# Mixing a paged decode into a dense FFN: six steps per half cache, three score bursts, quarter and paired products

## The chip, the core and the metric

The kernel runs on one core of one Trainium2 chip. The time is the device time of one execution in microseconds. Three runs of the kernel before took 1327.28, 1329.06 and 1329.76 us; the median, 1329.06 us, is what a later time is compared with. The kernel is one launch that computes everything from inputs in HBM to outputs in HBM. Five engines work side by side, each on its own queue of instructions: TensorE (PE in the profile, with its weight loads as PEld), VectorE (DVE), ScalarE (ACT), GpSimd (POOL) and SyncE (SP), which issues most DMAs. A semaphore makes one engine wait for another.

## What is computed

One layer of a hybrid decoder for two groups of tokens with shared weights: a prompt of 512 tokens, and a sample group of 8 sequences with 4 new tokens each, which attends to 4096 cached positions in pages of 128. All values are float32.

```python
h = h + 0.5 * rmsnorm(swiglu(rmsnorm(h, g0), wg[0], wu[0], wd[0]), g1)     # first FFN, width 2816
z = rmsnorm(h, g2) @ w_in                # HGRN2 group (4 heads) and MLA group (4 heads)
o_h = gated linear recurrence over z;    o_m = latent softmax attention over z and the cache
h = h + rmsnorm(concat(o_h, o_m) @ w_out, g3)
h = h + 0.5 * rmsnorm(swiglu(rmsnorm(h, g4), wg[1], wu[1], wd[1]), g5)     # second FFN

swiglu(x, wg, wu, wd) = (silu(x @ wg) * (x @ wu)) @ wd
# the sample group's attention, per sequence and head, over cached and new keys
s = (q_lat @ c_kv.T + q_rope @ k_rope.T) * scale;   p = softmax(masked s);   o = p @ c_kv
```

A cached position has a latent row of 256 numbers (both key and value) and a rotary key of 64. The pages of one sequence lie scattered in a pool and are found through a page table. The eight caches together are 42 MB.

## The kernel before, in words

**Layout.** Activations are held transposed: 128 features on the partitions, tokens along the free axis. The 544 tokens (512 of the prompt, 32 of the sample group) are two parts, `x = 0` with 256 columns and `x = 1` with 288, the sample tokens at its end.

**Dense products.** Each float32 weight tile is split into a high and a low float32r part by `weight` (line 219): SyncE loads `wraw` (512 KB, three buffers), ACT casts the high part `wh` (L237), DVE subtracts for the low part `wl` (L238). From the start of the second FFN four `wh`/`wl` pairs are in rotation (`NW` and `WX`). A product of a 128 x 128 tile is then three matmuls, and `gemm` (line 249, its matmuls at L246) runs all k tiles of a weight into one PSUM bank named `acc`, of which there are four. `gemm_q` (line 256) does the same as a generator and stops after every second k tile.

**The FFN as a generator.** `ffn` (line 297) runs the width of 2816 (22 columns of 128) in chunks of 6, 6, 5 and 5 columns for the second FFN. For each column j it makes the gate product, the up product, the SwiGLU product on DVE and ACT (L318 to L321) and its split into `hh` and `hl` (L158, L159), and yields: 48 matmuls per step for one part. After a chunk's columns come eight down products, one per 128 rows of the output, each over the chunk's 6 or 5 k tiles (18 or 15 matmuls), and each yields. The last k tile of a down product is the column that the chunk made last. So part 0 of the second FFN (`gb`, line 1016) is 22 + 32 = 54 steps.

**The decode as a generator.** The caches are worked in 16 halves (`Half`, line 1072), two for each of the 8 sequences. For a half:

- `gather` (line 1078): four indirect DMAs on POOL's queue bring two groups of 128 x 8 latent rows (`craw`, 1 MB each, in six slots of old activations: ulb, uhb, ha, hb, mb, q0) and their rotary keys (`rraw`, four buffers).
- `turn` (line 1097): DVE turns the keys of both groups in 32 x 32 blocks into `kh` (L1102, L1103). `KHB = 2` buffers of 10 KB per partition: both hold one half.
- `score` (line 1106, matmuls at L1115): 80 small matmuls, ten j by eight, on quarters of the array (64 rows by 32 columns), each two in the trace; then the row maxima `mxd`, `mxh` on DVE.
- `peak` (line 1126, PE at L1128, then DVE), `weigh` (line 1135, the exponential on ACT at L1138), `place` (line 1140: the weights turned and copied into `pbuf`).
- `value` (line 1148, matmuls at L1154): 16 matmuls, two each in the trace, of the weights with the latent rows; and `gathered` (line 1160, L1165), every second half, to collect the result.

`decode` (line 1168) runs them as a pipeline over halves. In a round n it gathers half n, turns half n - 1, scores, peaks, weighs and places half n - 2, and makes the values of half n - 3, in four yields: the first five j of the scores; the last five j, the values and the gather; the peak and the whole turn; the weights.

**What sets the order.** Lines 1244 to 1256 mix the two generators: 43 steps of the FFN (`DRATE = 0.8` of 54) over 79 steps of the decode, in even proportion. That gives the order in which instructions are traced. A planner then puts each engine's queue in order: it goes by the traced order, and where an instruction would have to wait by its own estimate, it takes a later one that is ready. An engine then works off its queue strictly in that order. `decode_new` (line 1028), the attention to the new tokens themselves, is a third generator stepped along with the decode.

**Behind it.** The 11 FFN steps that are left (three columns and eight down products) fill gaps in the output projection of part 1: `FILL = (4, (7, 8, 9), (1, 2, 3, 4), 4)` gives 4 steps before it, one at each of three places in it, and 4 behind it (line 1355 on).

Of the kernel before, what the change touches and what calls it, by code (L numbers as in the profile page):

```python
# [8 lines left out]
F32 = mybir.dt.float32  # L9
# [8 lines left out]
P = 128  # L18
# [20 lines left out]
ROWS = 8  # L39
# [11 lines left out]
W0 = 0  # L51
JOBS = (0, 1, 2, 6, 7, 8, 3, 4, 5)
CQ, NST = (0, 0, 0, 3, 1), 3
FILL = (4, (7, 8, 9), (1, 2, 3, 4), 4)
PTB, PEB, QNB = 2, 3, 1
LEP, LXP, EB, XB = (), (), 2, 2
PAT = (2, 2, 2, 2, 2, 2, 2, 3, 4, 2, 2, 3, 2)
PATL = (2, 1, 2, 1, 2, 1, 2, 2, 3, 1, 1, 2, 1)
NW, WX = 2, 2
DRATE = 0.8  # L60
KHB = 2
LEVELS = (32, 16, 8, 4, 2, 1)
CH = 64

# [39 lines left out]
def hybrid_step_kernel(  # L104
# [148 lines left out]
        mm3(acc[:, :n], [((wh[:, k], wl[:, k]), (act_[0][:, k], act_[1][:, k])) for k in range(kt)])  # L253
        return acc[:, :n]

    def gemm_q(wt, act_):
        wh, wl, kt = wt
        acc = ps("acc", "acc")
        n = act_[0].shape[-1]
        for k in range(kt):  # L260
            if k and k % 2 == 0:
                yield
            for i, (a, b) in enumerate(((wh, act_[0]), (wh, act_[1]), (wl, act_[0]))):
                nc.tensor.matmul(acc[:, :n], a[:, k], b[:, k], start=k + i == 0, stop=k == kt - 1 and i == 2)  # L264
        return acc[:, :n]

    def wcols(w, k0, kt, c0, n=P):
        return w[k0 * P : (k0 + kt) * P, c0 : c0 + n].rearrange("(k p) f -> p k f", p=P)
# [28 lines left out]
    def ffn(i, n_post, xs, u, nxt=None, mid=None, late=None, fin=None, pre=()):  # L297
        pool = cur[-1]
        yield
        r2 = {x: u[x][2] for x in xs}  # L300
# [50 lines left out]
        if mid:  # L351
            mid()
        for p in ends:
# [659 lines left out]
    ffa = ExitStack()  # L1013
    wx.append(ffa.enter_context(scope("ffa")))
    seam = []
    gb = ffn(1, 5, (0,), u4, late=lambda: rstd_u(u4[0], 0), pre=seam)
    next(gb)

    with scope("dec"):
# [45 lines left out]
        pbuf = mk([P, 2, 2, ROWS, 32], F32, "pbuf")  # L1065
        nc.gpsimd.memset(pbuf, 0.0)
        NH2 = 2 * NB
        NS = 3 * NH2 + 11

        PTG = {"ulb": 0, "uhb": -1, "ha": -1, "hb": 1, "mb": 0, "q0": -1}  # L1070

        class Half:
# [21 lines left out]
                    self.craw.append(craw)  # L1094
                    self.rraw.append(rraw)

            def turn(self):
                self.kh = []
                for g in range(2):
                    kh = mk([P, ROWS, 10, 32], F32, "kh", KHB)  # L1100
                    for a in range(0, ROWS, 4):
                        nc.vector.transpose(kh[:, a : a + 4, :8].rearrange("p a j k -> p a (j k)"), self.craw[g][:, a : a + 4])  # L1102
                    nc.vector.transpose(kh[:, :, 8:].rearrange("p a j k -> p a (j k)"), self.rraw[g])  # L1103
                    self.kh.append(kh)

            def score(self, js):
                q = qbd[self.b % 2]
# [59 lines left out]

        def decode():
            H = {}
            for t in range(NS):  # L1170
                n, r = divmod(t, 3)

                def at(k):
                    return H.get(n - k)

                if n < NH2 and r == 0:
                    H[n] = Half(n)
                if r == 0:
# [5 lines left out]
                    if at(2):  # L1184
                        at(2).score(range(5, 10))
                    if at(3):
                        at(3).value(H.get(n - 4))
                    if n >= 3 and at(0):
                        at(0).gather()
                    yield  # L1190
                elif r == 1:
                    if at(2):
                        at(2).peak()
                    if at(1):
                        at(1).turn()
                    yield
                else:
                    if at(3):
                        at(3).gathered()
                    if at(2):  # L1200
                        at(2).weigh()
                    yield
                    if at(2):
                        at(2).place()
                H.pop(n - 5, None)

        def decode_end():
# [36 lines left out]
        next(ga)  # L1244
        na, nb = NS + (NS + 2) // 3, int((22 + 32) * DRATE)
        ia, ib = 1, 0
        while ia < na:
            if ia * nb <= ib * na:
                next(ga, None)
                next(gn, None)  # L1250
                ia += 1
            else:
                next(gb, None)
                ib += 1
        for _ in ga:
            pass
# [162 lines left out]
```

## Time and profile before

| what | value |
|---|---|
| median of three runs | 1329.06 us |
| the profiled execution's own time | 1329.72 us |
| its span, first to last instruction | 1327.9 us |
| granted TensorE clock, mean | 0.991 |
| decode and second FFN mixed | about 745 to 1019 us |
| first and last score matmul | 784.5 and 1007.5 us |
| instructions of scores, values | 2560, 512 matmuls |

How to read it: the page gives each engine's busy time and share of the span; busy tenths in 40 slices of 33 us; the chain of work that ended last; and the costliest groups of instructions. Rows of the views name line, engine, operation and tiles as `out<-in`. A matmul's duration is longer than its distance to the next, since matmuls overlap; what counts is the distance from start to start. "issue" is a wait for which the profile shows no semaphore. Span and profiled time differ by 1.8 us that lie outside the first and last instruction.

### The profile page before, as it was taken

Reading aid. Unit: us, or ns where it says so; the run is one execution under the profiler, and the core shown is the slowest. Engines: PE = TensorE matmul, PEld = TensorE weight load, DVE = VectorE, ACT = ScalarE, POOL = GpSimd, SP = SyncE. Lnnn points to the kernel's source line nnn. Section 1 sums busy time; section 2 is a strip of 40 time slices with the busy share of each in tenths; the row PEclk is TensorE's granted clock in tenths of the full one; section 3 lists DMA queues with packets and bytes.
Section 4 is the critical chain, followed back from the end, with each engine's and each line's share of the span. In section 5 each row is a group of like instructions: output and inputs, shape, how many; then the busy total and the mean of one; then the engine's idle time right before and its main releaser. Section 6 shows DMA issues by size and latency. Waiting matters only on the chain.

```text
span 1327.9 us, 30474 instructions
## 1 busy us (share of the span) xinstructions
PE 1285.0 (97%) x12696; PEld 1205.2 (91%) x12696; DVE 888.4 (67%) x1782; ACT 697.7 (53%) x1454; POOL 76.7 (6%) x79
## 2 busy tenths in 40 slices
PE   7999999999999999999999899999899999999997
PEld 7999999999999988888888787877788999999996
DVE  7553245434558887786766878989888768566664
ACT  6543244224456754445658654554445677554454
POOL 0000000000000000000000413323210000000000
PEclk9999999999999999999999999999899999999998
DMA  6223232233244313233232869968768545656452
GB/s 187 84 84 92 82 94 81 82 95 95 76 131 128 110 52 97 81 87 115 74 96 77 313 202 285 312 213 312 256 212 262 153 134 166 180 152 181 140 167 70
DMA packets 280552, 192.87 MB, mean 145 GB/s; under 512 B 12765, under 2 KB 271422, under 8 KB 275550
## 3 DMA queue, kind: packets, MB, share of 16 engines
q1 hardware_dynamic: 271968, 147.85, 38.3%
q0 software_dynamic: 7168, 41.95, 8.4%
q8 instruction: 100, 1.64, 0.5%
q10 hardware_dynamic: 1278, 1.12, 0.3%
q14 instruction: 38, 0.31, 0.1%
HBM read 181.22 MB, written 9.67 MB: 144 GB/s over the span
## 4 chain that ended last, share of the span: by engine, by line
PE 83%; DVE 8%; ACT 4%; issue 2%; DMA 2%; SPq 0%; DVEq 0%; ACTq 0%
PE acc L246 61%; PE acc L264 9%; PE s L1115 3%; PE o L1154 2%; DVE kh L1102 2%; PE s L919 1%; DVE wl L238 1%; ACT wh L237 1%; PE pa L658 1%; PE zx L551 1%; DMA wraw<-w_u 1%; PE pr L179 1%; DMA xt<-x_p 1%; DVE ssq L173 0%; DMA wraw<-w_o 0%
## 5 line engine op out<-in xcount | busy, mean ns | idle before, releaser
L237 ACT CAST wh<-wraw 128x1024 fp32r<-128x1024 f32 (+3 forms) x255 | 248.4, 976 | 330.7 <-PE acc L246 266.8
L238 DVE TENSOR_TENSOR wl<-wraw,wh 128x1024 fp32r<-128x1024 f32 (+3 forms) x255 | 288.6, 1133 | 147.5 <-ACT wh L237 146.8
L246 PE MATMUL acc<-uhb,wh 128*128 128x288 f32 x768 | 228.3, 297 | 0.8 <-ACT uhb L195 0.8
L246 PE MATMUL acc<-ulb,wh 128*128 128x288 f32 x768 | 227.8, 297 | 0.0
L246 PE MATMUL acc<-uhb,wl 128*128 128x288 f32 x768 | 226.3, 295 | 1.2 <-DVE wl L238 1.2
L246 PE MATMUL acc<-uha,wh 128*128 128x256 f32 x768 | 220.6, 288 | 4.0 <-ACT wh L237 2.5
L246 PE MATMUL acc<-uha,wl 128*128 128x256 f32 x768 | 217.3, 284 | 1.8 <-DVE wl L238 1.7
L246 PE MATMUL acc<-ula,wh 128*128 128x256 f32 x768 | 217.4, 284 | 0.6 <-DVE ula L196 0.6
L246 PEld LDWEIGHTS acc<-uha,wh 128*128 128x128 f32 x768 | 145.6, 190 | 9.1 <-ACT wh L237 3.3
L246 PEld LDWEIGHTS acc<-uha,wl 128*128 128x128 f32 x768 | 145.5, 190 | 3.0 <-DVE wl L238 3.0
L246 PEld LDWEIGHTS acc<-uhb,wl 128*128 128x128 f32 x768 | 145.0, 189 | 1.7 <-DVE wl L238 1.7
L246 PEld LDWEIGHTS acc<-ula,wh 128*128 128x128 f32 x768 | 145.5, 190 | 1.1 <-DVE ula L196 1.0
L246 PEld LDWEIGHTS acc<-uhb,wh 128*128 128x128 f32 x768 | 144.7, 188 | 1.6 <-ACT uhb L195 1.0
L246 PEld LDWEIGHTS acc<-ulb,wh 128*128 128x128 f32 x768 | 144.7, 188 | 0.1
L246 PE MATMUL acc<-hlb,wh 128*128 128x288 f32 x317 | 93.8, 297 | 0.0
L246 PE MATMUL acc<-hhb,wh 128*128 128x288 f32 x317 | 93.4, 297 | 0.0
L246 PE MATMUL acc<-hhb,wl 128*128 128x288 f32 x317 | 92.9, 294 | 0.0
L246 PE MATMUL acc<-hha,wh 128*128 128x256 f32 x297 | 87.0, 293 | 5.5 <-ACT hha L158 4.2
L246 PE MATMUL acc<-hla,wh 128*128 128x256 f32 x297 | 84.5, 285 | 1.1 <-DVE hla L159 1.1
L246 PE MATMUL acc<-hha,wl 128*128 128x256 f32 x297 | 84.5, 285 | 0.0
L321 DVE TENSOR_TENSOR sil<-sil,acc 128x256 f32<-128x256 f32 (+1 forms) x88 | 38.2, 436 | 49.5 <-PE acc L246 47.4
L320 DVE TENSOR_TENSOR sil<-sil,sit 128x256 f32<-128x256 f32 (+1 forms) x88 | 38.5, 440 | 43.0 <-ACT sit L295 42.7
(476 smaller groups left out, 2767.4 us busy)
## 6 DMA issues: line engine op xcount, KB each, us to landing
wraw<-w_g SPq DMA_DIRECT2D x66, 512.0 KB, 4.0
wraw<-w_u SPq DMA_DIRECT2D x66, 512.0 KB, 3.8
wraw<-w_in SPq DMA_DIRECT2D x24, 512.0 KB, 3.8
wraw<-w_d SPq DMA_DIRECT2D x32, 384.0 KB, 3.8
wraw<-w_d SPq DMA_DIRECT2D x32, 320.0 KB, 3.3
wraw<-w_o SPq DMA_DIRECT2D x16, 512.0 KB, 4.1
wraw<-w_d SPq DMA_DIRECT2D x16, 448.0 KB, 3.7
wraw<-w_d SPq DMA_DIRECT2D x8, 512.0 KB, 4.0
```

The lines of the kernel that those rows point to most:

```text
L179: nc.tensor.matmul(pr[:, :n], ones, acc, start=True, stop=True)
L237: nc.scalar.copy(wh[:, :kt], w[:, :kt])
L238: nc.vector.tensor_tensor(wl[:, :kt], w[:, :kt], f32(wh[:, :kt]), op=ALU.subtract)
L246: nc.tensor.matmul(out, a, b, start=n == 0, stop=n == last)
L264: nc.tensor.matmul(acc[:, :n], a[:, k], b[:, k], start=k + i == 0, stop=k == kt - 1 and i == 2)
L320: nc.vector.tensor_tensor(s, s, t, op=ALU.mult)
L321: nc.vector.tensor_tensor(s, s, up[x], op=ALU.mult)
L551: nc.tensor.matmul(z, w[a][:, k], U[1][b][:, k], start=k + n == 0, stop=k == KD - 1 and n == 2)
L658: nc.tensor.matmul(pa[es, c * 32 : (c + 1) * 32].rearrange("p (n m) -> p n m", m=m), kx[:, cs], up(qx[:, cs]), start=True, stop=True, skip ...
L1102: nc.vector.transpose(kh[:, a : a + 4, :8].rearrange("p a j k -> p a (j k)"), self.craw[g][:, a : a + 4])
L1115: nc.tensor.matmul(self.s[r][c * 32 : c * 32 + 32, :P], q[rs, j], kh, start=j == 0, stop=j == 9, skip_group_check=True)
L1154: nc.tensor.matmul(o[g : g + 32, :R], self.p[:, c, a], self.craw[c][:, a], start=i + c == 0 and a < 4, stop=i + c == 2 and a >= 4, skip_gr ...
```

## The change

The edits, as one change:

- `decode` has six yields in a round instead of four: scores of three, three and four j, each its own step; the values and the gather; the peak; the weights. `turn` takes a group: group 0 in the step of the second score burst, group 1 in the step of the peak. In the first three rounds the gather stands in the first step, as before.
- `KHB` goes from 2 to 3. The scratch that holds POOL's DMA descriptors is set to 4096 bytes per partition (16384 by default), so 12288 bytes of each partition are free for other tiles; a buffer of turned keys has 10240.
- `gemm_q` takes a step size, and `ffn` a mode `fine`, used for part 0 of the second FFN alone. In it the gate and the up product each yield in the middle (after 4 of 8 k tiles, 12 matmuls) and at their end: four yields per column.
- In `fine`, except in the last chunk, the first two down products are made side by side by the new `gemm_2`: all k tiles but the last of the first, then of the second, a yield, then the last k tile of each.
- The mixing loop runs 6 x 19 = 114 decode steps and `NDEC = 100` FFN steps of the 120 that there are now; `decode_new` steps with every second decode step. 20 FFN steps stay for later, which are the same three columns and eight down products as before: `FILL` begins with 13 instead of 4.

```diff
-FILL = (4, (7, 8, 9), (1, 2, 3, 4), 4)
+FILL = (13, (7, 8, 9), (1, 2, 3, 4), 4)
-DRATE = 0.8
-KHB = 2
+NDEC = 100
+KHB = 3
...
-    def gemm_q(wt, act_):
+    def gemm_q(wt, act_, step=2):
...
-            if k and k % 2 == 0:
+            if k and k % step == 0:
                 yield
...
+    def gemm_2(wts, act_):
+        kt = wts[0][2]
+        n = act_[0].shape[-1]
+        accs = [ps("acc", "acc")[:, :n] for _ in wts]
+        for ks in (range(kt - 1), (kt - 1,)):
+            for (wh, wl, _), acc in zip(wts, accs):
+                for k in ks:
+                    for i, (a, b) in enumerate(((wh, act_[0]), (wh, act_[1]), (wl, act_[0]))):
+                        nc.tensor.matmul(acc, a[:, k], b[:, k], start=k + i == 0, stop=k == kt - 1 and i == 2)
+            if len(ks) > 1:
+                yield
+        return accs
...
-                ga = {x: gemm(wg_, u[x]) for x in xs}
+                ga, up = {}, {}
+                for x in xs:
+                    ga[x] = (yield from gemm_q(wg_, u[x], 4)) if fine else gemm(wg_, u[x])
+                if fine:
+                    yield
...
-                up = {x: gemm(wu_, u[x]) for x in xs}
+                for x in xs:
+                    up[x] = (yield from gemm_q(wu_, u[x], 4)) if fine else gemm(wu_, u[x])
...
-                wts = {d: pre.pop(0) if pre else weight([wcols(w_d[i], f0, nf, d * P)], nf, len(grp) > 1) for d in grp}
+                if fine and not last and grp[0] == 0:
+                    accs = yield from gemm_2([weight([wcols(w_d[i], f0, nf, d * P)], nf) for d in (0, 1)], (hh[xs[0]], hl[xs[0]]))
+                elif fine and not last and grp[0] == 1:
+                    accs = accs[1:]
+                else:
+                    accs = None
+                wts = None if accs else {d: pre.pop(0) if pre else weight([wcols(w_d[i], f0, nf, d * P)], nf, len(grp) > 1) for d in grp}
...
-                        acc = gemm(wts[d], (hh[x], hl[x]))
+                        acc = accs[0] if accs else gemm(wts[d], (hh[x], hl[x]))
...
-                yield
+                if not accs or grp[0] == 0:
+                    yield
...
-    gb = ffn(1, 5, (0,), u4, late=lambda: rstd_u(u4[0], 0), pre=seam)
+    gb = ffn(1, 5, (0,), u4, late=lambda: rstd_u(u4[0], 0), pre=seam, fine=True)
...
-            def turn(self):
-                self.kh = []
-                for g in range(2):
-                    kh = mk([P, ROWS, 10, 32], F32, "kh", KHB)
...
+            def turn(self, g):
+                if g == 0:
+                    self.kh = []
+                kh = mk([P, ROWS, 10, 32], F32, "kh", KHB)
...
         def decode():
             H = {}
-            for t in range(NS):
-                n, r = divmod(t, 3)
+            for n in range(NH2 + 3):
...
+                for r, js in enumerate((range(3), range(3, 6), range(6, 10))):
                     if at(2):
-                        at(2).score(range(5))
-                    if n < 3 and at(0):
+                        at(2).score(js)
+                    if r == 0 and n < 3:
                         at(0).gather()
+                    if r == 1 and at(1):
+                        at(1).turn(0)
                     yield
...
+                if at(3):
+                    at(3).value(H.get(n - 4))
+                if n >= 3 and at(0):
+                    at(0).gather()
+                yield
+                if at(2):
+                    at(2).peak()
+                if at(1):
+                    at(1).turn(1)
+                yield
+                if at(3):
+                    at(3).gathered()
+                if at(2):
+                    at(2).weigh()
+                yield
+                if at(2):
+                    at(2).place()
...
-        na, nb = NS + (NS + 2) // 3, int((22 + 32) * DRATE)
...
+        na, ib = 6 * (NH2 + 3), 0
+        for ia in range(na):
+            next(ga)
+            if ia % 2:
                 next(gn, None)
-                ia += 1
-            else:
-                next(gb, None)
+            while ib * na < (ia + 1) * NDEC:
+                next(gb)
                 ib += 1
...
-    nc = _bacc.Bacc("TRN2", target_bir_lowering=False, num_devices=1)
+    nc = _bacc.Bacc("TRN2", target_bir_lowering=False, num_devices=1, dynamic_dma_scratch_size=4096)
```

More of the change, by code (lines that the diff above doesn't have):

```diff
@@ L295, in sigmoid, with ffn @@
         nc.scalar.activation(out, out, AF.Exp, scale=-1.0)
-    def ffn(i, n_post, xs, u, nxt=None, mid=None, late=None, fin=None, pre=()):
+    def ffn(i, n_post, xs, u, nxt=None, mid=None, late=None, fin=None, pre=(), fine=False):
         pool = cur[-1]
@@ L1067, in hybrid_step_kernel @@
         NH2 = 2 * NB
-        NS = 3 * NH2 + 11
         PTG = {"ulb": 0, "uhb": -1, "ha": -1, "hb": 1, "mb": 0, "q0": -1}
@@ L1095, in gather @@
                     self.rraw.append(rraw)
-            def turn(self):
-                self.kh = []
-                for g in range(2):
-                    kh = mk([P, ROWS, 10, 32], F32, "kh", KHB)
[L1101 to L1104, printed above, removed]
+            def turn(self, g):
+                if g == 0:
+                    self.kh = []
+                kh = mk([P, ROWS, 10, 32], F32, "kh", KHB)
+                for a in range(0, ROWS, 4):
+                    nc.vector.transpose(kh[:, a : a + 4, :8].rearrange("p a j k -> p a (j k)"), self.craw[g][:, a : a + 4])
+                nc.vector.transpose(kh[:, :, 8:].rearrange("p a j k -> p a (j k)"), self.rraw[g])
+                self.kh.append(kh)
             def score(self, js):
@@ L1169, in decode @@
             H = {}
-            for t in range(NS):
-                n, r = divmod(t, 3)
+            for n in range(NH2 + 3):
                 def at(k):
                     return H.get(n - k)
-                if n < NH2 and r == 0:
+                if n < NH2:
                     H[n] = Half(n)
-                if r == 0:
+                for r, js in enumerate((range(3), range(3, 6), range(6, 10))):
                     if at(2):
-                        at(2).score(range(5))
-                    if n < 3 and at(0):
+                        at(2).score(js)
+                    if r == 0 and n < 3:
                         at(0).gather()
+                    if r == 1 and at(1):
+                        at(1).turn(0)
                     yield
[L1184 to L1196, printed above, removed]
-                else:
[L1198 to L1204, printed above, removed]
+                if at(3):
[15 more added lines that the diff above has]
+                    at(2).place()
                 H.pop(n - 5, None)
@@ L1243, in hybrid_step_kernel @@
         ga, gn = decode(), decode_new()
-        next(ga)
-        na, nb = NS + (NS + 2) // 3, int((22 + 32) * DRATE)
[L1246 to L1249, printed above, removed]
+        na, ib = 6 * (NH2 + 3), 0
+        for ia in range(na):
+            next(ga)
+            if ia % 2:
                 next(gn, None)
-                ia += 1
-            else:
-                next(gb, None)
+            while ib * na < (ia + 1) * NDEC:
+                next(gb)
                 ib += 1
```

## The prediction

> **What bounds the kernel now.** First the page: its busy rows, slices and chain.
>
> ```profile
> span 1327.9 us, 30474 instructions
> PE 1285.0 (97%) x12696; PEld 1205.2 (91%) x12696; DVE 888.4 (67%) x1782; ACT 697.7 (53%) x1454; POOL 76.7 (6%) x79
> ...
> PE   7999999999999999999999899999899999999997
> ...
> PE 83%; DVE 8%; ACT 4%; issue 2%; DMA 2%; SPq 0%; DVEq 0%; ACTq 0%
> ```
>
> PE sets the end: 83% of the chain. PE's work is not reduced by this change (the same matmuls run), so the only things to win are its idle time, its lost clock and the cost of changing between kinds of work. POOL's gathers and the decode lie in slices 23 to 31, so next the table by stretches, with the whole stage in which decode and the second FFN are mixed (745 to 1019) and its two slowest-clocked pieces.
>
> ```profile
> 745.00:1019.00 274.00, 254.40 (x4394) 217.66 (x4392) 239.25 (x527) 139.91 (x364) 66.26 (x59) 0.98 0.80 264
> 880.00:900.00 20.00, 17.68 (x284) 14.63 (x282) 15.93 (x39) 10.92 (x30) 4.23 (x4) 0.91 0.64 201
> 940.00:960.00 20.00, 17.22 (x276) 14.22 (x275) 15.17 (x32) 8.91 (x23) 4.54 (x4) 0.83 0.79 262
> ```
>
> The columns are length, PE, PEld, DVE, ACT and POOL busy, clock, DMA share, GB/s. In 274 us PE is idle 274 - 254.4 = 19.6 us, and a clock of 0.98 costs another 5.5. This is all the stage holds for PE. DVE is busy 239.25 us, leaving 34.75 free: it stands close behind PE. DMA engines are busy 0.80 of the time. Then PE's waits there (740 to 1030):
>
> ```profile
> PE s L1115 <- issue: 8.4, 6, 2.8
> PE acc L246 <- ACT wh L237: 2.5, 3, 1.8
> PE acc L246 <- ACT hha L158: 2.3, 3, 1.7
> PE s L1128 <- DVE mxh L1124: 1.6, 4, 0.8
> PE acc L246 <- issue: 1.3, 1, 1.3
> PE acc L246 <- DVE hla L159: 1.1, 2, 0.6
> PE acc L246 <- DVE wl L238: 1.0, 2, 0.8
> ...
> PE o L1154 <- issue: 0.6, 1, 0.6
> ```
>
> Half of it, 8.4 + 1.3 + 0.6 = 10.3 us, is "issue": no semaphore explains it. The chain of waits shows where, and the DMA views what moves then (whole run; 745 to 784; 925 to 950):
>
> ```profile
> 836.52 1.86 PE o L1154 x32
> ...
> 850.64 2.40 PE s L1115 x160
> ...
> 925.26 2.38 PE s L1115 x111
> 927.64 2.48 issue
> 930.13 0.42 PE s L1115 x7
> ...
> 935.32 5.78 PE acc L246 x48
> 941.10 2.16 PE s L1115 x143
> 943.26 2.78 issue
> ```
>
> ```profile
> q8 instruction: 100, 1.64, 0.5%
> ```
>
> ```profile
> q8 instruction: 2, 0.03, 0.3%
> ```
>
> ```profile
> q8 instruction: 4, 0.07, 1.1%
> ```
>
> A score matmul takes 2.40/160 = 15 ns, a dense one 5.78/48 = 120 ns. PE's code comes as 100 packets of 16.4 KB for 2 x 12696 instructions: one block is 127 load and matmul pairs, 15 us of dense work but 1.9 us of scores. A half has 160 score matmuls and 32 value matmuls in one stretch, and the gap opens after 110 to 140 of them. I read "issue" as the wait for the next block, in a DMA system 80% busy.
>
> [...]
>
> **The change, part by part.** *Scores in three bursts (24, 24 and 32 matmuls, each two in the trace: 48, 48, 64) with a piece of dense work between, and dense products in halves of 12 matmuls.* Six steps per half, 19 halves, 114 steps for 100 pieces: 0.88 piece a step. From the first score to the end of the values PE now issues 160 + 32 + 4 x 0.88 x 12 = 234 pairs, in 160 x 0.015 + 1.9 (values, the row of 1.86) + 42 x 0.12 = 9.3 us, so a block lasts some 5 us instead of 1.9; the stalls show that a block needs at most about 1.9 + 2.8 = 4.7. The waits go away, and the clock lost after the longest of them: 20 x (1 - 0.83) = 3.4 us. Together 10.3 + 3.4 = 13.7; bounds 0 and 13.7. I take 80%, since a step without a piece (12%) joins two bursts: -11.0.
>
> [...]
>
> *First two down products side by side.* At each of the three seams inside the stage the first product stops at its last k, whose input is the newest SwiGLU column:
>
> ```profile
> 887.70 0.28 PE L246 MATMUL acc<-hha,wl 128*128 128x256 f32 x1
> 889.66 0.39 PE L246 MATMUL acc<-hha,wh 128*128 128x256 f32 x1 [1.68 <-ACT hha L158]
> 890.69 0.49 PE L246 MATMUL acc<-hla,wh 128*128 128x256 f32 x1 [0.64 <-DVE hla L159]
> ```
>
> Now 15 matmuls of the second product (12 in the last chunk) stand ahead of it, 15 x 0.12 = 1.8 us. The waits on hha and hla are 2.3 + 1.1 = 3.4 us, the clock after them 20 x (1 - 0.91) = 1.8. The longest (2.32) keeps 0.5; I take -2.9 and half the clock, -0.9: -3.8, bounds 0 and -5.2. Price: two weight pairs held instead of one, of four.
>
> *More turns between dense and decode work.* One such turn, a half whose keys come late:
>
> ```profile
> 898.10 0.28 PE L246 MATMUL acc<-hha,wl 128*128 128x256 f32 x1
> 898.31 0.41 PE L1115 MATMUL s<-kh,q 64*32 64x128 f32 x4
> 898.65 0.39 PE L246 MATMUL acc<-hha,wh 128*128 128x256 f32 x1
> ```
>
> From start to start 0.55, less one dense pitch 0.12, less four scores 0.06: 0.37 us; the clean x160 stretch pays it once, halves split by late keys five times. I count 4 x 0.88 = 3.5 turns a half after, about 2.7 before (between one and five, nearer one): 0.8 x 16 x 0.3 = +4; bounds 0 (splits vanish) and (3.5 - 1) x 16 x 0.37 = +15.
>
> *Third kh buffer, turn in two parts.* DVE's work, from its groups in 745 to 1018, and the gathers' landing after issue (740 to 1030):
>
> ```profile
> L1103 DVE STREAM_TRANSPOSE kh<-rraw 128x512 f32<-128x512 f32 x32 | 22.2, 693 | 0.0
> L1102 DVE STREAM_TRANSPOSE kh<-ulb 128x1024 f32<-128x1024 f32 x12 | 14.8, 1234 | 1.4 <-PE s L1115 1.4
> ```
>
> ```profile
> rraw<-pool_r,idx POOLq DMA_INDIRECT x32, 7.0
> ...
> ha<-pool_c,idx POOLq DMA_INDIRECT x5, 7.5
> ...
> uhb<-pool_c,idx POOLq DMA_INDIRECT x5, 8.9
> ```
>
> One turn of both groups is 4 x 1.23 + 2 x 0.69 = 6.3 us; in two parts, 3.2 each, other DVE work passes between. The first part no longer waits for the previous scores (the 1.4 above is such a wait). It covers PE's 1.6 on mxh at best. But the gather stands in step 4 and the first turn in step 2 of the next half, four steps of about 274/19/6 = 2.4 us = 9.6 us, against 7.5 to 8.9 us of landing: the slack is about 1 us. On DVE's queue weight lows, SwiGLU products and maxima stand behind a turn that waits, and PE stands behind those. I take 0; bounds -1.6 and +23 (a rival below).
>
> *Finer mix.* Before, 43 pieces go into 79 steps, 2.2 a half, of 48 x 0.12 = 5.8 or 18 x 0.12 = 2.2 us; now 5.3 a half, of 1.4 or 2.2. The first score stands behind 12 x 0.88 / 4 = 2.6 gate and up columns instead of 8 x 43/79 = 4.4, and the first weights meet the first gathers harder. PE's waits on wh and wl, 2.5 + 1.0 = 3.5, may go or double: 0, bounds -3.5 and +3.5. The pieces left after the stage hold the same matmuls (13 + 3 + 4 quarter or whole steps for 4 + 3 + 4): 0; cover is PE's own queue.
>
> *Smaller descriptor scratch.* POOL's issues:
>
> ```profile
> L1093 POOL DMA_INDIRECT rraw<-pool_r,idx x32 | 40.2, 1258 | 66.0 <-DVE kh L1103 57.9 <-DVE q L1166 3.4 <-issue 2.3
> ```
>
> POOL idles 66 us before these alone, so even a doubled issue (another 40 us) is covered: 0. Were the cover gone it would delay the landing, the same rival.
>
> **The sum.** -11.0 - 3.8 + 4 = -10.8. The profiled execution took 1329.72 (span 1327.9 and 1.8 around it), 0.66 over the median 1329.06; so 1318.9 for it and 1318.3 on the median. I say 1318, range of this case 1311 to 1325.
>
> **Rivals.** *All waits go* (0.14): issue, clock, seams, mxh and the start, 13.7 + 5.2 + 1.6 + 3.5 = 24.0 of the 25.1 that the stage holds, with +3 for turns: 1329 - 21 = 1308. For it: DVE's 34.75 us free. Against: DVE would have to be 239/253 = 95% busy without ever holding PE up.
>
> *The bursts change nothing* (0.14): the issue gaps are not code blocks, or the planner lets bursts run together as it does today with two half scores (x160 above). Then -3.8 + 4 = 0: 1329. [...] Against: gaps of the same place and size, always inside scores or values.
>
> *DVE waits for the gathers* (0.26): with a buffer free early, the planner puts the first turn behind the second turn of the half before (step 5) rather than at its own place. That is 2.4 + 3.2 = 5.6 us after the gather's issue, where the latents land after 7.5 to 8.9 and the key rows, issued one POOL instruction (1.26) later, after 1.3 + 7.0 = 8.3. With 8.6: 3 us of waiting at the head of DVE's queue. DVE has 34.75/19 = 1.8 us free a half, 1.25 in a stage 11 us shorter. In 10 of the 13 halves gathered inside the loop: 10 x (3 - 1.25) = +17.5, less 10.8: +7, 1336. It decides from a wait of about 2.3 us a half. For it: DVE's load. Against: none of DVE's waits in the stage before names a gather.
>
> **How the numbers follow.** The forecast has 0.46. Under 0.2% (2.7 us) a measurement of this kernel can't tell a change. Faster: 0.46 + 0.14 + 0.04 of the third case = 0.64; same: 0.10 of it; slower: 0.26. The range 1306 to 1338 takes in the forecast, most of the first and half of the last rival, about 0.82.
>
> **What would show it.** Right: issue waits before L1115 and L1154 under 3 us together, no 20 us stretch of the stage below 0.95, hha and hla waits under 1.5, score groups of 48 to 64 in PE's order, the stage 10 us shorter. Wrong: a DVE wait before kh on a gather, more than 64 turns, issue gaps that stay though the bursts are apart.

## The result, and the profile after

The changed kernel took 1336.09 us in the median (1332.37 to 1338.02), the kernel before 1329.06: a ratio of 1.0047 with a 95% interval of 1.0034 to 1.006. It is slower, by 6.2 us on that ratio; the forecast was 10.8 us faster. The execution that was profiled took 1332.37 us, the fastest of these runs, so its trace shows a smaller loss than the median.

The page after, first its span and engines, then the slices of PE and the chain of work that ended last:

```profile
span 1330.6 us, 30465 instructions
PE 1286.0 (97%) x12696; PEld 1204.8 (91%) x12696; DVE 888.4 (67%) x1782; ACT 698.3 (52%) x1454; POOL 77.0 (6%) x79
...
PE   7999999999999999999999888989999999999997
...
PE 77%; DVE 11%; DMA 6%; ACT 4%; issue 2%; SPq 0%; DVEq 0%; ACTq 0%; POOLq 0%
```

The same matmuls run, and DVE's and ACT's totals are the same within 0.6 us. What differs is the chain: PE had 83% of it and has 77; DVE went from 8 to 11 and DMA from 2 to 6. The end is now reached by way of transfers and DVE more often. The stage in which decode and the second FFN are mixed, and its two slowest-clocked slices (columns as in the prediction):

```profile
745.00:1019.00 274.00, 254.79 (x4361) 218.04 (x4361) 236.09 (x510) 138.45 (x353) 67.24 (x59) 0.98 0.79 260
800.00:820.00 20.00, 15.75 (x266) 13.43 (x267) 13.83 (x33) 8.38 (x24) 5.13 (x5) 0.91 0.68 225
820.00:840.00 20.00, 17.25 (x281) 15.11 (x280) 15.80 (x34) 9.65 (x28) 5.77 (x4) 0.91 0.90 303
```

PE's busy time in these 274 us was 254.40 and is 254.79, at the same clock: no idle time was won, and 33 fewer matmuls fit in (4361 for 4394). PE's waits in the stage (740 to 1045; total us, times, longest):

```profile
PE s L1152 <- DVE mxh L1148: 9.7, 5, 3.0
PE acc L264 <- DVE wl L238: 4.2, 4, 2.6
PE s L1139 <- issue: 2.7, 2, 2.5
PE s L1139 <- ACT q L1162: 1.8, 1, 1.8
...
PE o L1178 <- issue: 0.2, 1, 0.2
```

The row that the change aimed at did what was forecast: "issue" fell from 10.3 us to 2.7 + 0.2, and the waits on hha and hla (3.4) are gone from the list. In their place stands the wait for the row maxima (L1148, before L1124), 1.6 before and 9.7 now, and that for wl, 1.0 before and 4.2 now. Both are made by DVE, though DVE is less busy (236.09 for 239.25). So the next question is what DVE's queue waits for, and behind it ACT's. First ACT before, then ACT after, then DVE after:

```profile
ACT wh L237 <- DMA wraw<-w_u: 7.9, 2, 6.3
```

```profile
ACT wh L237 <- DMA wraw<-w_u: 17.8, 6, 4.3
...
ACT wh L237 <- DMA wraw<-w_d: 11.1, 8, 3.6
...
ACT wh L237 <- DMA wraw<-w_g: 4.8, 5, 1.3
```

```profile
DVE wl L238 <- ACT wh L237: 13.9, 12, 3.1
...
DVE kh L1126 <- DMA ha<-pool_c,idx: 2.3, 3, 1.3
DVE kh L1126 <- DMA ulb<-pool_c,idx: 2.2, 2, 1.1
DVE kh L1126 <- DMA mb<-pool_c,idx: 1.8, 2, 1.0
```

Two kinds of waiting on transfers stand behind this. ACT stands 33.7 us before casts whose raw weights have not landed; before, its waits that name a weight load were 7.9 + 2.3 + 0.7 = 10.9 us (w_u, w_d, w_g), so this kind is not new but three times as large. And DVE stands 6.3 us before turns whose latents have not landed, where no wait of DVE's named a gather before. The chain of waits shows how each reaches PE (start, length, what). First the gather of half 8:

```profile
877.99 7.80 DMA mb<-pool_c,idx
...
885.81 1.25 DVE kh L1126
...
894.23 1.24 DVE kh L1126
895.47 0.37 DVE mxd L1146 x2
895.84 1.15 DVE kh L1126
896.99 0.05 DVE mxh L1148
...
897.09 0.80 PE s L1152 x2
```

The transfer ends at 885.79 and the first turn starts 0.02 us later; the next turn, 894.23, is in DVE's queue ahead of the maxima and partly between their two steps, and PE's peak at 897.09 has waited for it. Then the end of the decode:

```profile
1011.39 6.78 DMA wraw<-w_u
...
1018.27 1.05 ACT wh L237
...
1019.34 1.23 DVE wl L238
1020.57 0.41 DVE mxd L1146 x2
...
1021.00 0.17 DVE mxh L1148
...
1021.22 0.49 PE s L1152 x2
```

Here a wait "for the maxima" is a weight that came late: its low part stands ahead of the maxima in DVE's queue, and DVE stood 3.08 us before it (1016.26 to 1019.34), though the scores that the maxima read had ended at 1015.44. One name in PE's list, two causes; the experiments separate them.

### The profile page after: what moved, and what is told of

Its sections match the earlier page's. It is cut to its first block, busy times and chain, and to the rows that moved or that the text cites. A ratio compares the mean times of both kernels' runs of the same rounds, so it can differ in the third digit from the quotient of the medians.

```text
span 1330.6 us, 30465 instructions
## 1 busy us (share of the span) xinstructions
PE 1286.0 (97%) x12696; PEld 1204.8 (91%) x12696; DVE 888.4 (67%) x1782; ACT 698.3 (52%) x1454; POOL 77.0 (6%) x79
## 4 chain that ended last, share of the span: by engine, by line
PE 77%; DVE 11%; DMA 6%; ACT 4%; issue 2%; SPq 0%; DVEq 0%; ACTq 0%; POOLq 0%
PE acc L246 52%; PE acc L264 13%; DVE wl L238 2%; DVE kh L1126 2%; DMA wraw<-w_u 2%; PE s L944 1%; ACT wh L237 1%; PE s L1139 1%; DMA mb<-pool_c,idx 1%; PE pa L683 1%; PE o L1178 1%; DMA wraw<-w_g 1%; PE zx L576 1%; DVE pbuf L1170 1%; PE pr L179 1%
## 5 line engine op out<-in xcount | busy, mean ns | idle before, releaser
L264 PE MATMUL acc<-uha,wh 128*128 128x256 f32 x528 | 159.4, 302 | 1.4 <-ACT wh L237 0.9
L264 PE MATMUL acc<-uha,wl 128*128 128x256 f32 x528 | 150.2, 285 | 4.2 <-DVE wl L238 4.2
L264 PE MATMUL acc<-ula,wh 128*128 128x256 f32 x528 | 150.5, 286 | 0.6 <-DVE ula L196 0.6
L246 PE MATMUL acc<-uha,wh 128*128 128x256 f32 x416 | 118.2, 284 | 1.0 <-DVE sil L336 1.0
L246 PE MATMUL acc<-uha,wl 128*128 128x256 f32 x416 | 117.6, 283 | 0.8 <-DVE wl L238 0.8
L246 PE MATMUL acc<-ula,wh 128*128 128x256 f32 x416 | 117.5, 282 | 0.0
L264 PEld LDWEIGHTS acc<-uha,wh 128*128 128x128 f32 x528 | 101.0, 191 | 14.8 <-issue 11.3
L264 PEld LDWEIGHTS acc<-uha,wl 128*128 128x128 f32 x528 | 100.7, 191 | 5.4 <-DVE wl L238 5.2
L264 PEld LDWEIGHTS acc<-ula,wh 128*128 128x128 f32 x528 | 101.1, 192 | 2.0 <-DVE ula L196 1.0
L246 PEld LDWEIGHTS acc<-uha,wh 128*128 128x128 f32 x416 | 78.5, 189 | 1.4 <-DVE sil L336 1.2
L246 PEld LDWEIGHTS acc<-uha,wl 128*128 128x128 f32 x416 | 78.4, 188 | 1.4 <-DVE wl L238 1.4
```

What stands on the lines that cost most here:

```text
L246: nc.tensor.matmul(out, a, b, start=n == 0, stop=n == last)
```

## Experiments

The theory after this reading: (1) with an even mix, three raw weight buffers (`wraw`) let the dense loads arrive late among the gathers; (2) the third buffer of turned keys lets the planner put the first turn where the gather has barely landed. Rivals: the order of turns and maxima on DVE alone; the place where the turn or the gather is written; the finer pieces or the bursts as such. All times below are ratios to the kernel before, run on the same chip, with 95% intervals.

### Each part alone

*e1*: the finer dense pieces and paired down products on the old four-step decode, with two buffers of turned keys. In this kernel one dense step fewer runs in the stage, so the last chunk's down products take each other's weights and one output is not the layer's; the amount of work is the same (12696 matmuls), and e11 below repeats the run with all steps and with the weights in their places.

```diff
-        na, nb = NS + (NS + 2) // 3, int((22 + 32) * DRATE)
+        na, nb = NS + (NS + 2) // 3, NDEC
```

> The finer dense pieces and the paired first down products alone, with the decode, the turns and the two kh buffers of before; 100 pieces over the 79 old decode steps. Theory G (the early first turn holds DVE at gathers that have not landed, so maxima and with them PE come late): the dense part is not the fault, so no slower than before, 1322 to 1330. Rival D (the even mix itself is the fault: decode begins earlier, weights and gathers meet in the first 50 us): 1332 to 1338, with PE waits on wh and wl. Rival S (each turn between dense and decode work costs more than estimated): about 1329, since scores stay in two bursts; more than 3 us of issue waits at the scores remain.

Measured 0.9994 (0.998 to 1.0008). PE's waits:

```profile
PE s L1153 <- DVE mxh L1149: 17.8, 7, 4.6
PE s L1140 <- issue: 1.0, 2, 0.6
```

The fine pieces alone take most of the issue waits away (1.9 us left, with 0.6 before L1265 and 0.3 before L1153): the dense pieces now stand between the two half scores. What they won was lost to maxima that come late, 17.8 us, which no expectation had.

*e2*: the six-step decode with three bursts alone; dense steps, turn (whole, in the step of the peak) and buffers as before.

```diff
-DRATE = 0.8
+NDEC = 43
...
+                for r, js in enumerate((range(3), range(3, 6), range(6, 10))):
...
+                if at(1):
+                    at(1).turn()
```

> The six-step decode with three score bursts alone: whole turn in the step of the peak, two kh buffers, the 43 whole dense steps of before over 114 decode steps. Theory G: issue waits fall only in part, since 0.38 coarse pieces a step leave bursts joined; 1325 to 1330. Rival S: 1332 or more. Rival D: as before, 1327 to 1330.

Measured 1.0068 (1.005 to 1.0087), 1338.33 us, as rival S had it and in the median slower than the whole change (the intervals overlap). Issue waits are still 4.4 + 2.9 + 2.9 us (before scores, values and dense products), ACT waits 14.1 us for w_u and 4.5 for w_d, PE 7.8 for the maxima. The bursts by themselves neither remove the issue waits nor cost nothing.

### The third buffer of turned keys

*e3*: the changed kernel with the whole turn in the step of the peak, two buffers of turned keys and the default descriptor scratch.

```diff
-KHB = 3
+KHB = 2
...
-                    if r == 1 and at(1):
-                        at(1).turn(0)
...
-                    at(1).turn(1)
+                    at(1).turn()
```

> The changed kernel with the whole turn back in the step of the peak, two kh buffers and the default scratch: bursts and fine dense pieces stay. Theory G: no DVE wait on a gather, PE's wait on mxh under 4 us, issue waits under 3 us, time 1318 to 1326. Rival S or D: what is left is what costs, 1333 to 1338. If two kh buffers are too few, PE waits on kh at the scores instead and the time lies above 1336.

Measured 1.0006 (0.999 to 1.0022). No wait of DVE's names a gather any more; the wait for the maxima is 6.8 us. Taking this part back returns 0.41%, less than theory G had expected (1329.49 us instead of 1318 to 1326), and ACT's waits for weights stay:

```profile
ACT wh L237 <- DMA wraw<-w_u: 18.7, 5, 6.7
```

*e4*: the changed kernel with the second turn held behind the maxima in DVE's order, so that a late turn can't delay them.

```diff
+                    with tc.issue_after(at(2).mxi.ins) if at(2) else nullcontext():
+                        at(1).turn(1)
```

> The changed kernel with one edge more: the second turn of a half stands behind the maxima (mxh) of the half being scored on DVE's queue. Theory G: the wait of PE at the peak on mxh (9.7 us in five) falls to under 3 us and the time by 5 to 10 us, to 1326 to 1331; DVE's 6.3 us of waits on gathers stay. Rivals S and D: within 3 us of the changed kernel, 1333 to 1338.

Measured 1.0044 (1.0028 to 1.006): the same as the changed kernel, so the gain that theory G expected did not come. PE's waits moved instead of going:

```profile
PE acc L264 <- DVE wl L238: 5.9, 3, 5.2
PE s L1139 <- ACT q L1162: 4.3, 4, 1.8
PE s L1139 <- issue: 3.2, 4, 2.6
PE s L1152 <- DVE mxh L1148: 2.7, 2, 2.1
```

The wait for the maxima fell from 9.7 to 2.7 us, and those for wl, the exponential and the queries (2.6 us on DVE's L1190) rose. That the second turn's place ahead of the maxima is by itself the cause falls with this run: put behind them, it holds up others. ACT's waits for weights are not shorter (36.9 us for 33.7); DVE's waits for gathers are 3.0 us instead of 6.3, and that did not help either.

*e5*: e3 with three buffers of turned keys again (and the small scratch that makes room): only the buffer comes back, not the early place of the turn.

```diff
-KHB = 2
+KHB = 3
```

> The changed kernel with the whole turn in the step of the peak, but with its three kh buffers and the small descriptor scratch. It parts the place of the turn from the third buffer and the scratch. Theory G (the early place of the first turn costs the last 5 us, by DVE standing at gathers): as with the late turn and two buffers, ratio to before 0.998 to 1.003. Rival K (with a third buffer the planner pulls turns forward wherever they stand in the text, or the small scratch slows the gathers): as the changed kernel, 1.004 to 1.007, with DVE waits on gathers.

Measured 1.0054 (1.0035 to 1.0072), like the changed kernel. PE's wait for the maxima, then DVE's waits:

```profile
PE s L1152 <- DVE mxh L1148: 15.5, 7, 4.2
```

```profile
DVE kh L1126 <- DMA ha<-pool_c,idx: 2.3, 3, 1.0
DVE kh L1126 <- DMA ulb<-pool_c,idx: 1.8, 2, 1.0
DVE kh L1126 <- DMA mb<-pool_c,idx: 1.7, 3, 0.8
```

So it isn't where the turn is written. With a buffer free, the planner takes the turn as soon as it reckons the keys there: in e5 the first turns of 13 halves start within 3 us of the landing of their latents, eight of them within 0.1 us. In the kernel before, the gather of the same halves has landed 0.9 to 17.5 us before the turn, and in e3, which differs from e5 by the buffer and the scratch alone, 4.3 to 12.6 us. The small scratch does not explain it: in the runs that have it with two buffers of turned keys, the gathers land as soon after their issue as with the large one (median 7.87 us in e8 for 7.91 before, 7.70 in e7 for 7.71 in e3).

*e15*: the kernel before with a third buffer of turned keys and scratch 4096, nothing else.

```diff
-KHB = 2
+KHB = 3
```

> The kernel before with a third buffer of turned keys and descriptor scratch 4096, nothing else. If a buffer that is free early makes the planner put the first turn at the gather's landing whatever the mix, DVE shows waits of kh on gathers (before: none) and the time is 0.2 to 0.5% over the kernel before. If the buffer hurts only in the finer mix, where DVE has less to do between, the time is within 0.15% of before and DVE's waits on gathers stay under 2 us.

Measured 1.0028 (1.0013 to 1.0043): slower by itself, in the coarse mix too. PE's waits, then DVE's:

```profile
PE s L1128 <- DVE mxh L1124: 7.9, 6, 2.1
```

```profile
DVE kh L1102 <- DMA ulb<-pool_c,idx: 2.8, 3, 1.1
DVE kh L1102 <- DMA ha<-pool_c,idx: 1.8, 2, 1.5
...
DVE kh L1102 <- DMA mb<-pool_c,idx: 0.5, 1, 0.5
```

There are 5.1 us of gather waits where there were none, and 7.9 us for the maxima instead of 1.6. This is the third rival's mechanism without the finer mix, and far smaller than the rival had it.

### The gather earlier

*e6*: values and gather moved behind the first burst, to give the gather three steps more.

```diff
+                    if r == 0 and at(3):
+                        at(3).value(H.get(n - 4))
+                    if r == 0 and n >= 3 and at(0):
+                        at(0).gather()
...
-                if at(3):
-                    at(3).value(H.get(n - 4))
-                if n >= 3 and at(0):
-                    at(0).gather()
```

> The changed kernel with the values and the gather three steps earlier, behind the first score burst, so that seven steps instead of four lie between a gather and its first turn. Theory G: DVE's waits on gathers (6.3 us) vanish and the ratio falls from 1.0047 to 0.997 to 1.002. Rival W (weights that land late hold ACT's casts, then DVE's wl, the maxima and PE): ratio stays at 1.003 to 1.007, ACT's waits on weight loads (33.7 us in the changed kernel) stay above 25 us.

Measured 1.0278 (1.0256 to 1.0301), the worst, and outside both expectations; DVE still waits 6.7 us for gathers. The values now come before their weights are placed (PE waits 10.6 us for pbuf in 10 places), the maxima cost 14.9 us, and the casts wait 31.5 us for w_d, 17.9 for w_g and 12.1 for w_u. The room for the latents is free only after the values have read it, so the gather can't be had earlier without the values. A failed remedy; it tells nothing on the two causes.

### More raw weight buffers

*e8*: the kernel before with five raw weight buffers and scratch 4096. *e7*: e3 with the same. *e9*: the changed kernel with four (scratch 2048, to make room). *e13* and *e12*: e3 with four and with six, scratch 4096.

```diff
-        w = mk([P, 8, P], F32, "wraw", 3, pool=sb)
+        w = mk([P, 8, P], F32, "wraw", 5, pool=sb)
```

> The kernel before with the small scratch and five wraw buffers, nothing else. Rival W holds for the kernel before too if this is faster: its waits of ACT on weight loads and the issue gaps before casts were 20.8 us; 0.993 to 0.998. Theory D2: 0.998 to 1.002. If the small scratch slows the gathers: above 1.002, with POOL issues longer than 1.26 us on average.

> The late turn with two kh buffers again, and the room of the small scratch used for five wraw buffers instead of three, so that weight loads are issued two weights earlier. Rival W: ACT's wait on weight loads (22 us with three) falls under 8 us, PE's wait on mxh under 3 us, and the time by 6 to 12 us, to a ratio of 0.991 to 0.996. Theory D2 (DVE is simply full: 236 us busy in 274 and in order, so any wait taken away comes back as another): ratio 0.998 to 1.002.

> The changed kernel, its three kh buffers and early turn included, with four wraw buffers instead of three (the descriptor scratch goes to 2048 bytes to make room). Rival W as the whole cause: the loss is gone, ratio 0.992 to 0.997. Rival K beside W (a third buffer lets the planner put the first turn ahead of its gather's landing, and that costs by itself): the ratio falls, but stays 0.3 to 0.6% above that of two kh buffers with five wraw (0.991), 0.994 to 1.000, and turns still start within 0.1 us of a landing.

> The changed kernel with the whole turn in the step of the peak, two buffers of turned keys and four raw weight buffers (descriptor scratch 4096). The changed kernel with four raw buffers stood at 0.9987. If the third buffer costs by itself and the two costs add, this run is 0.41% under that: about 0.9946, and PE's wait for the maxima falls from 4.8 us to 3 or 4. If the third buffer hurts only where weights are late too, this run is 0.9975 to 0.999.

> The late turn with two kh buffers and six wraw buffers. Rival W: with five, ACT's waits on weight loads were nearly gone, so a sixth adds little: 0.989 to 0.992. If 0.986 or less, loads were still late with five.

```
raw weight buffers                  3                     4                     5                     6
kernel before                     1.0                     -    0.9956 (.9943-.9970)                   -
three kh buffers (changed)     1.0047    0.9987 (.9970-1.0005)                    -                   -
two kh buffers (late turn)     1.0006    0.9926 (.9905-.9946)  0.9910 (.9891-.9929)   0.9894 (.9873-.9915)
```

Weights that land in time are worth 0.44% to the kernel before and 0.96% to the late turn, most of it with the fourth buffer; the fifth and sixth are each within the intervals. At four buffers, three kh instead of two cost 0.61% (0.9987 / 0.9926; e9 has half of e13's scratch besides), where they cost 0.41% at three: within the intervals the two causes add, and each stands without the other. With four raw buffers DVE still waits 9.8 us for gathers in e9, and not at all in e13. In e7 little is left of PE's waits, and ACT's for weights are 4.3 us on w_u, where e3 had 18.7, and 1.5 on w_g:

```profile
PE s L1152 <- DVE mxh L1148: 3.3, 2, 1.7
...
PE s L1139 <- issue: 1.3, 1, 1.3
```

```profile
ACT wh L237 <- DMA wraw<-w_u: 4.3, 1, 4.3
```

e8 keeps 9.8 + 1.2 us of issue waits on PE, so the buffers don't touch those. ACT's waits before casts for which no semaphore shows, which the expectation of e8 counted with the weights, were 12.9 us before and stay at 11.7 in e8; those that name a load go from 10.9 to 2.3.

### Bursts or fine pieces, with the weights in time

*e10*: e2 with five raw buffers. *e11*: e1 with five, and all 100 dense steps run. *e14*: e11 without the paired down products. All with scratch 4096.

```diff
+        while ib < NDEC:
+            next(gb)
+            ib += 1
```

> The six-step decode alone (1.0068 with three wraw buffers), with the small scratch and five wraw buffers. Rival W: its loss was weights that came late, so 0.995 to 0.999, near the kernel before with five (0.9956). Rival S (bursts cost by their turns between dense and decode work): 1.000 to 1.004, still 0.5 to 0.9% above the kernel before with five.

> The fine dense pieces and paired down products alone, decode in four steps and two kh buffers as before, with the small scratch and five wraw buffers; all 100 pieces are run out ahead of the decode's end. If the gain of the late turn with five wraw (0.991) is that of bursts and fine pieces together, this lies between 0.991 and 0.9956. Rival: the fine pieces give all of it, 0.990 to 0.992, and the bursts nothing.

> The fine pieces on the four-step decode with five raw weight buffers (0.9849), but each down product by itself again. If the pairs carry what the prediction gave them (3.8 us, 0.29%), this run is about 0.988 and PE's waits on hha and hla at the seams come back, 2 to 3 us; if the broken-up scores carry all of it, 0.985 and the seam waits stay under 1 us.

Measured 0.9946 (0.9925 to 0.9967), 0.9849 (0.9824 to 0.9873) and 0.9868 (0.9846 to 0.989). Against e8 (0.9956) the bursts alone are within the intervals, the fine pieces with the pairs win 1.07%, more than either expectation had, and without the pairs 0.88%; the difference between the last two, 0.19%, is within the intervals. In e14 one wait on hha comes back, 1.6 us, also between what its two expectations had. Putting the bursts on top of the fine pieces (e7, 0.9910) costs 0.62%. e11 is the best kernel of the study, 1310.70 us in the median for 1329.33 of the kernel before in the same runs: fine pieces and pairs on the old four-step decode, two kh buffers, five raw ones. Its stage and its waits:

```profile
745.00:1019.00 274.00, 260.93 (x4509) 227.69 (x4509) 249.41 (x550) 150.33 (x382) 61.95 (x60) 0.99 0.85 277
```

```profile
PE s L1153 <- DVE mxh L1149: 7.7, 7, 2.3
PE s L1140 <- issue: 1.9, 2, 1.0
```

115 more matmuls fit into the stretch than before. What the bursts cost on top can be counted from the starts of PE's matmuls between the first score and the last value. Decode work here is scores, peaks, values and their collecting; a change is a dense matmul followed by one of decode, or the reverse. From each distance of two starts the ordinary one is taken off, 0.12 us after a dense matmul and 0.014 us after one of decode, except in the last column but one, which is a plain sum. Distances over 0.4 us are in the last column alone.

```
                      stretch   changes   at changes   dense to dense   decode to decode   over 0.4 us
before                  233.3       114      12.6 us          5.2 us           71.9 us        23.8 us
changed                 263.4       156      18.1            10.7              69.2           23.4
e11 (fine, 5 raw)       239.9       116      12.7             5.5              71.2           13.2
e7  (+ bursts, 5 raw)   249.3       156      17.9             6.8              71.2           11.3
```

From e11 to e7 that is 5.3 + 1.3 + 0 - 1.9, or 4.7 us (nearly all the rest of the 9.4 us by which the stretch is longer are 38 dense matmuls more in it): the bursts save 1.9 us of long gaps and pay 6.6 for more changes and slower dense neighbours. The ratios give 8.2 us (0.62%), uncertain by 3 to 4; what the count doesn't hold lies outside this stretch or within that uncertainty, and stays open. The fine pieces alone hardly add changes (116 for 114); the bursts on top of them add 40.

## Why the prediction was wrong, step by step

Two terms that the prediction put at nothing are the steps that failed, the finer mix and the third buffer of turned keys, and the turns between dense and decode work were taken too few. The ratios form a chain from the kernel before to the changed one, with the terms of the prediction as its links (1% is 13.3 us; each link has an uncertainty of some 0.2 to 0.3%, 3 to 4 us, so the sum closes by construction, but each size is rough):

```
term of the prediction            forecast (bounds)       measured as                         us
issue, clock and seams            -14.8 (-18.9 to 0)      e11 against e8                   -14.3
more turns between kinds           +4   (0 to +15)        e7 against e11                    +8.2
finer mix, weights and gathers      0   (-3.5 to +3.5)    (e3 against e7) less (1 / e8)     +7.0
third kh buffer, turn in two        0   (-1.6 to +23)     changed against e3                +5.4
sum                               -10.8                                                     +6.3
```

- **The issue waits and the seams** were right in size, and by a different part than the prediction named: it gave them to the bursts and the half pieces together, and the half pieces alone do it (e1, e11). So the close agreement is partly luck. The bursts alone leave 0.6 + 3.0 + 2.2 = 5.8 us of issue in e10. "No 20 us stretch below 0.95" was wrong: 0.91 from 800 to 840. The rival that the gaps have another cause than code fell. The trace's DMA records show it: each of the six issue gaps over 0.4 us before (9.6 of the 10.3 us) ends 1.27 to 1.47 us after the end of a 16384-byte packet on q8 (the packet from 943.47 to 944.58 us, PE again from 946.04), and so does the one that is left in the changed kernel, 1.32 us after it. Between 745 and 1019 us q8 brought 35 such packets in the kernel before, and six of them end ahead of one of these gaps. When dense work is mixed into the scores, 10.3 us of waits go to 2.9. The gap that is left, in the chain of the changed kernel, where two bursts ran together:

```profile
802.07 1.58 PE s L1139 x94
803.65 1.62 PE acc L264 x12
805.27 0.78 PE s L1139 x37
806.04 2.49 issue
```

  94 + 12 + 37 = 143 matmuls in 4 us, a little over the 127 pairs to a packet that the prediction worked out from 100 packets for 12696 pairs, and PE stands for 2.49 us.

- **Paired down products** were given 3.8 us; e14 says 0.19%, 2.5 us, which the intervals don't separate from none. In the changed kernel the seam waits are gone, as forecast.

- **The finer mix** is the first step that failed: put at 0, it measures +7.0 us, outside its bounds of 3.5, though four ratios go into that figure and 3 to 4 us of it are uncertain. What the runs showed in its place: with three raw buffers the weights of the even mix land too late, and five buffers give 0.96% back where they give the kernel before 0.44%. The term was sized from PE's waits on wh and wl (3.5 us), taken as all that late weights can cost. A late weight need not show there: at the end of the decode above the load took 6.78 us, DVE stood 3.08 us before the low part of that weight, and PE's wait of 2.30 us names the maxima that stand behind it. The row of ACT before (7.9 us on w_u) and its gain with five buffers (0.44%, 5.8 us) show that the cost was there already; the prediction sized the term by PE's row alone.

- **The third buffer** is the second: it was taken at 0 and costs 5.4 us, with the mechanism of the loss written out as a rival and the range reaching over it. That rival's mechanism was right in kind (first turns at the landing, maxima behind them) and wrong in size: 6.3 us of DVE waiting instead of 30, 5.4 us instead of 17.5, and no threshold of 2.3 us a half: 6.3 us over ten halves is 0.6, and it cost already. How the early turn costs is shown only in part. PE's waits for the maxima rise with the buffer (6.8 to 15.5 us from e3 to e5, 1.6 to 7.9 in e15), but in e4 neither shorter waits for gathers nor the second turn's place behind the maxima gave anything back. The gain that was its upper bound, 1.6 us of waiting for maxima that goes, was not seen. That the rival's 1336 us is the measured time is luck: it came by three terms and not by the one.

- **The turns** lay within their bounds, at twice the size taken by the ratios. By the count, two changes to a turn, the kernel before has 57 turns and the changed one 78, where the prediction had 43 and 56; the 21 more cost 5.5 us at the changes (12.6 to 18.1), 0.26 us each, so the price (0.3) was about right and the number too low.

- **The scratch** was costed at nothing, and no cost is seen: e8 has a quarter of the default and is faster than the kernel before, e9 an eighth and is faster than the changed one. It was not tried by itself, but the gathers land as soon with it (7.87 us in e8 for 7.91 before).

With the weights in time and two buffers of turned keys, so without the two terms that were put at nothing, the change is worth e7 against e8, 0.46% or 6 us: the sign of the forecast with a bit over half its size.

## What to carry to other kernels

Before costing a mix at nothing, follow each engine's waits one engine back: PE's row names the last engine that was late, and here late weights stood behind the waits of two other engines, 33.7 us of ACT's on loads and 13.9 us of DVE's on wh in the changed kernel. A spare buffer is not free where a planner fills queues by its own estimate of when data land: give it to the loads that are late (here raw weights) rather than to work that then runs as early as it can. When several parts of a change win by the same mechanism, try the smallest alone; here, with the weights in time, the half pieces had all of the gain and the bursts only their cost.

## What the runs showed of the hardware that was not expected

In the changed kernel the granted clock was 0.91 over two neighbouring slices (800 to 840) with no PE wait longer than 2.8 us there, and in the kernel before 0.83 over 940 to 960, where the longest was 2.78 us. In the traces of the kernel before, the changed one, e8 and e11, all 15 issue gaps over 0.4 us in the stage end 1.27 to 1.48 us after the end of a 16384-byte code packet. In the changed kernel a 512 KB weight tile of the up or gate product takes 4.9 and 5.7 us in the median from issue to landing between 740 and 1030 us, beside 4.0 and 4.4 over the whole run, and the chain of the kernel before with a third kh buffer (e15) holds 9.86 us of a smaller tile, for w_d (384 or 320 KB in this stage).
